# A hybrid decoder layer on one core: filler matmuls moved from the attention to the merge and the joint tiles behind it

## The chip, the cores and the metric

The kernel runs on one core of a Trainium2 chip. The metric is the device time of one execution in microseconds (us); the median of three runs is given. The core has a matmul engine (TensorE, here PE, with its weight loads shown as PEld), VectorE (DVE), ScalarE (ACT), GpSimd (POOL), SyncE (SP, which issues most transfers) and 16 DMA engines. PE accumulates into PSUM banks of 128 x 512 fp32; DVE and ACT read them from there. Each engine works through its own instructions in order and waits on semaphores for the others.

## The reference

The reference is one layer of a decoder for 1024 tokens and 1024 channels: an RWKV-7 path and a sparse attention path side by side, merged by sigmoid gates, then a SwiGLU FFN with 2816 hidden channels (22 tiles of 128) and a final RMSNorm. Cut to what matters here:

```
u    = rmsnorm(x, norm1_g);  proj = u @ w_in
y_a  = rwkv7_mix(...);       y_b  = dsa_attention(...)
merged = g_a * (y_a @ w_o_rwkv) + g_b * (y_b @ w_o_att)
h = x + merged @ w_out
z_gate, z_up = split(rmsnorm(h, norm2_g) @ w_ffn_in)
h = h + (silu(z_gate) * z_up) @ w_ffn_out
out = rmsnorm(h, normf_g)
```

## The kernel before

**Products.** Every fp32 operand is split into a rounded high part and a rest (`split`, L116: ACT makes the high part in L117, DVE subtracts it in L118). A product is the sum hi x hi + hi x lo + lo x hi, so an output tile of 128 channels x 512 tokens with eight blocks of 128 channels in is 24 matmuls. `mm3` (L138) issues them in the order of L143, L144, L148 and yields the number of matmuls after each few. `mm3_last` (L152) does several tiles at once and keeps the last input block for the end. Weights come by SP into the ring `wst` (three buffers), and their parts into `whi` and `wlo` (two each). The PSUM pool `acc` has three banks, the pool `mix` five. The ring `tmp` has four buffers of 128 x 512.

**Halves.** The tokens are worked on in two halves of 512. The second half is late: its attention has to end before its merge can start. The first half's FFN is therefore used as filler beside the second half's attention.

**The filler.** `fill` is a queue of generators. `pump(n)` adds n to a credit and takes steps from the queue until the credit is used up; each step takes off the number of matmuls it yielded. A generator that has just yielded stands still there, and what it would do next (to read its PSUM banks, for example) is issued only when it is pumped again. `run_over` runs a generator and pumps -n for each negative yield. PE's order is the order of the program, written out by hand in this way. The other engines are ordered by a planner, which works with estimated times, takes the earlier place in the program first, and puts rushed weights (`weights` with `rush`) ahead.

**The order around the change.** After the second RWKV half, 130 matmuls of filler are pumped. Then `attend(1)` runs over four pairs of heads with four blocks of 128 queries, 16 units. Per unit and head of the pair it makes the logits (L1082, reduced by DVE in L1084, exponential in L1087), transposes them (`turn`, L1096, copied by ACT in L1098) one unit later, and multiplies with the values (L1106) two units later. Each step yields a number that is pumped. At the end the sums go through DRAM (`close2` to `close4`: the transfer to d_s in L1131, back in L1137, the product L1142, the store to d_yb in L1143), with 6 pumped ahead of each step.

Then `merge(1)` loads both paths' results from DRAM (L1201), splits them, pumps 30, multiplies with w_o and the gates, pumps 10, multiplies with w_out into the residual h (L1236) and sums its squares (`Rms.add`, L250). It ends there for the second half.

The filler in this stretch is `ffn(0, ...)`: two groups of eight hidden tiles (`ffn_in`, 48 matmuls each, and then `ffn_out`, 192 matmuls, with the add of L1321 that reads each bank). While the second group's `ffn_out` runs, `scaled` multiplies the first half's z by its row of the norm, one block of 128 channels at a time (L1443, L1444, split, store to d_z in L1446).

**The joint tiles.** The last six hidden tiles are done by `joint` for both halves at once, with a scheme that needs seven block products where the plain way needs eight: sums and differences of weights (`s1` to `s4`, the ring `sw`) meet sums and differences of the two halves' activations. With h normed for the second half (L1540) and the first half's z read back from d_z (`old`, L1549), the mixed operands are T1 (L1556), T2 (L1571), T3 (L1570), B22 and T4 (L1580, L1581), each split into hi and lo. The first rows (`m1`, `m2`) need only the first half. Each tile j of six issues seven `product`s of 12 matmuls (L1505, L1506, L1508): Y with T1; m1 of tile j + 2; X with T2; Y with B22; X with T3; m2 of tile j + 2; X with T4. Copies by ACT (L1591 for m5, L1598 for u2) and adds by DVE (L1602, L1609) read the banks between products that go on in the same bank. What is left of the filler is issued in one go ahead of the first rows (`run(*fill)`).

**The output.** `reload` brings the joint tiles' results back for the first half. The second half's FFN becomes the filler (`ffn(1, ...)`), 48 are pumped, `ffn_out(0, ..., JOINT, sq0)` adds the last product of the first half, 60 more, `norm_out` writes the first half's output, and the rest of the filler and the second half's last product (`finish_out`) follow.

Of the kernel before, what the change touches and what calls it, by code (L numbers as in the profile page):

```python
# [27 lines left out]
JOINT = 2  # L28
# [22 lines left out]
def block_kernel(ctx: ExitStack, tc: tile.TileContext, ins: dict, outT: bass.AP, outR: bass.AP, stop=None, dbg=None):  # L51
# [126 lines left out]
    def pump(n):  # L178

        credit[0] += n  # L180
        while credit[0] > 0 and fill:
            try:
                credit[0] -= abs(next(fill[0]))
            except StopIteration:
                fill.popleft()
        if not fill:
            credit[0] = 0
# [857 lines left out]
    def attend(half, p, bias):  # L1045
# [112 lines left out]
        for i in range(len(units) + 2):  # L1158
            if i < len(units):
                hp, bi = units[i]  # L1160
                if i == 0:
                    kqv[hp] = load(hp)
                    load_q(hp, 0)
                    load_q(hp, 1)
                if bi == 2 and hp < 3:
                    kqv[hp + 1] = load(hp + 1, sms[hp][:, 0, :] if half else None)
                    load_q(hp + 1, 0)
                    load_q(hp + 1, 1)
                if bi == 0:
                    sms[hp] = smp.tile([128, 4, 2], F32, tag="sm", name="sm", bufs=3)  # L1170
                Ls[i] = []
            for e in range(2):
                if i < len(units):
                    Ls[i].append(logits(hp, bi, e, kqv[hp], sms[hp]))
                    yield 5 if half else (bi + 3) // 2
                if 0 <= i - 1 < len(units):
                    ptss.setdefault(i - 1, []).append(turn(units[i - 1][1], Ls[i - 1][e]))
                    yield 4 if half else (units[i - 1][1] + 3) // 2
            if i >= 2:
                hp2, bi2 = units[i - 2]  # L1180
                if bi2 == 0:
                    pys[hp2] = mix()
                values(bi2, ptss.pop(i - 2), kqv[hp2], pys[hp2])
                if bi2 == 3:
                    ri = close1(sms[hp2])
                yield 4 if half else bi2 + 1
                if bi2 == 3:
                    closing.append((2, hp2, ri))
                elif closing:
                    close(closing)  # L1190
# [5 lines left out]
    def merge(half, zp, zs, between=None):  # L1196
        yt = yhi, ylo = act_tiles(zp, "y", ("s0", "s1"))
        mt = act_tiles(zp, "m", ("s2", "s3"))
        for j in range(8):
            t = ylo[:, j, :].bitcast(F32)  # L1200
            SY.dma_start(t, (d_ya if j < 4 else d_yb)[half][j % 4])  # L1201
            split(yhi[:, j, :], ylo[:, j, :], t)
        yield -30
        for d in range(8):
            w = weights(ins["w_o"][d])
            ga, gb = tmp(), tmp()
# [218 lines left out]
    def ffn(half, zp, zs, tags, after=None):  # L1425

        for gi in range(JOINT):
            f = act_tiles(zp, "f", tags)
            yield from ffn_in(f, zs, gi)
            side = iter(after() if after and gi == JOINT - 1 else ())  # L1430
            for i, n in enumerate(ffn_out(half, zp, f, gi)):
                yield n
                if i % 2:
                    next(side, None)
            for _ in side:
                pass

# [20 lines left out]
    def parts(t):  # L1458
        return [t[:, k, :] for k in range(4)], [t[:, 4 + k, :] for k in range(4)]

    def joint(z0, zp0, zs1, zp1, md):


        g0, gn = GROUPS[JOINT]
# [65 lines left out]

        yield ahead
        h, sq = zs1
        sq.columns()
        pump(10)
        row = sq.row()
        pump(16)
        b11, b21 = ([[x[:, k, :] for k in ks] for x in z0] for ks in (range(4), range(4, 8)))

        def normed(k):
            V.scalar_tensor_tensor(h[:, k, :], h[:, k, :], par[:, P_N2 + k:P_N2 + k + 1], row,  # L1540
# [6 lines left out]
        def old(k):  # L1547
            t = tmp()
            SY.dma_start(t, d_z[k])  # L1549
            return t  # L1550

        t1, T1 = pair(zp1, "s2")
        for k in range(4):
            normed(k)
            x = old(k)
            V.tensor_tensor(x, h[:, k, :], x, op=ALU.subtract)  # L1556
            split(t1[:, k, :], t1[:, 4 + k, :], x)
        run(*fill)
        fill.clear()
        with tc.high_priority():  # L1560
            first_rows(0)
            first_rows(1)
        for j in range(2):
            m1(j)
            m2(j)
        (t2, T2), (t3, T3) = pair(zp1, "s3"), pair(zp0, "s2")
        for k in range(4):
            normed(4 + k)
            x, y = tmp(), old(k)
            V.tensor_tensor(x, h[:, 4 + k, :], h[:, k, :], op=ALU.subtract)  # L1570
            V.tensor_tensor(y, y, x, op=ALU.add)  # L1571
            split(t2[:, k, :], t2[:, 4 + k, :], y)
            split(t3[:, k, :], t3[:, 4 + k, :], x)
        b22, B22 = pair(zp1, "s1")
        for k in range(4):
            split(b22[:, k, :], b22[:, 4 + k, :], h[:, 4 + k, :])
        t4, T4 = pair(zp0, "s0")
        for k in range(4):
            x = old(4 + k)
            V.tensor_tensor(x, x, t2[:, k, :].bitcast(F32), op=ALU.subtract)  # L1580
            V.tensor_tensor(x, x, t2[:, 4 + k, :].bitcast(F32), op=ALU.subtract)  # L1581
            split(t4[:, k, :], t4[:, 4 + k, :], x)

        for j in range(gn):
            nxt, far = j + 1 < gn, j + 2 < gn
            if far:
                first_rows(j + 2)
            Y = acc()
            product(Y, w[j]["s1"], T1, True)
            m5 = tmp()  # L1590
            A.activation(m5, Y, AF.Copy)  # L1591
            if nxt:
                s1(j + 1)
            if far:
                m1(j + 2)
            product(X[j], w[j]["s2"], T2, False)
            u2 = md.tile([128, HT], F32, tag="u2", name="u2")
            A.activation(u2, X[j], AF.Copy)  # L1598
            if nxt:
                s2(j + 1)  # L1600
            product(Y, w[j]["s4"], B22, False)
            V.tensor_tensor(u2, u2, Y, op=ALU.add)  # L1602
            t = tmp()
            A.activation(t, u2, AF.Tanh, scale=0.5)
            if nxt:
                s4(j + 1)
            V.scalar_tensor_tensor(t, t, 1.0, u2, op0=ALU.add, op1=ALU.mult)
            product(X[j], w[j]["s3"], T3, False)
            V.tensor_tensor(m5, X[j], m5, op=ALU.add)  # L1609
            if nxt:  # L1610
                s3(j + 1)
            if far:
                m2(j + 2)
            V.scalar_tensor_tensor(t, m5, 0.5, t, op0=ALU.mult, op1=ALU.mult)
            SY.dma_start(d_f[1][j], t)
            product(X[j], w[j]["a22"], T4, False)
            V.scalar_tensor_tensor(f0[j], X[j], 0.5, f0[j], op0=ALU.mult, op1=ALU.mult)
            SY.dma_start(d_f[0][j], f0[j])
        t, B12 = pair(zp1, "s2")
        for k in range(4):  # L1620
            split(t[:, k, :], t[:, 4 + k, :], h[:, k, :])
        yield [Planes(*(a + b)) for a, b in zip(B12, B22)]

    def reload(half, f):
        for j in range(GROUPS[JOINT][1]):
# [85 lines left out]
    sb.close()  # L1711
    (sz1, zp1), zs1, sq0 = opened("right", "zp1"), [], []
    smd, md = opened("right", "md")
    stage_j = joint(z0[0], zp0, zs1, zp1, md)
    run_over(merge(1, zp1, zs1, next(stage_j)))
    z1 = next(stage_j)
    smd.close()
    fj = act_tiles(zp0, "f", ("s2", "s0"))
    reload(0, fj)
    fill.append(ffn(1, zp1, [z1, None], ("s3", "s0")))  # L1720
    pump(48)
    run_over(ffn_out(0, zp0, fj, JOINT, sq0))
    pump(60)
    run_over(norm_out(0, sq0[0]))
    pump(300)
    sz0.close()
# [88 lines left out]
```

## Time and profile before

| what | value |
|---|---|
| median of three runs | 1767.33 us (1766.26 to 1770.13) |
| the profiled execution | 1774.1 us, of which its span is 1772.2 us |
| mean granted PE clock | 0.984 |
| DMA | 253.45 MB in 148034 packets, 143 GB/s |
| second attention, first logits to last values | 980.65 to 1136.42 us |
| second merge, first to last dense matmul | 1153.67 to 1253.28 us |
| joint tiles, first row to the last product | 1278.67 to 1410.76 us |
| last product of the first half | 1421.64 to 1474.01 us |

Times within the profile are counted from the start of the span. In a timeline row the first number is the start, the second the length; a row may stand for several instructions (x4), and square brackets hold the idle time of the engine before it and what ended it. The length of a matmul is that of its way through the array, and the next one starts before it is over: the distance of the starts is what counts. In a row of the windows view stand the stretch, its length, the busy time and the number of instructions of each engine, the granted PE clock (1.00 is full), the DMA share and GB/s.

### The profile page before, as it was taken

The numbers are of one execution on the slowest core, as the hardware profiler recorded it, in microseconds if no ns is written. First come the engines' busy times: TensorE is split into PE (matmuls) and PEld (weight loads), VectorE is DVE, ScalarE is ACT, GpSimd is POOL, SyncE is SP. The second block draws the span as 40 slices with busy tenths as digits, with TensorE's granted clock in tenths as the row PEclk, the third lists the DMA queues.
The fourth block names the chain that finished last, engine by engine and source line by source line (L and its number), as shares of the span: only waits on it lengthen the run. The fifth ranks groups of instructions, "written<-read, shape, count | busy, mean of one in ns | idle before, by whom it ended". The sixth has DMA issues, their size and how long they took to land.

```text
span 1772.2 us, 26689 instructions
## 1 busy us (share of the span) xinstructions
PE 1708.6 (96%) x10000; PEld 1400.1 (79%) x10000; DVE 1147.6 (65%) x2238; ACT 871.4 (49%) x1685; POOL 104.5 (6%) x127
## 2 busy tenths in 40 slices
PE   8999999999999999999999999999989879999998
PEld 7888888888878777787878888767768757888887
DVE  6789899865577578678857555665686444433334
ACT  5365997543555888654243555433343332322322
POOL 0000000010022110001002110000000000000001
PEclk9999999999999999999999999999989999999999
DMA  5542344445376336632347553556522433353363
GB/s 212 184 133 78 108 110 144 146 129 155 111 220 183 114 122 200 202 108 93 115 127 214 147 155 102 177 186 203 171 77 86 162 111 122 126 170 112 112 192 104
DMA packets 148034, 253.45 MB, mean 143 GB/s; under 512 B 49681, under 2 KB 71889, under 8 KB 147777
## 3 DMA queue, kind: packets, MB, share of 16 engines
q1 hardware_dynamic: 123824, 176.53, 31.9%
q10 hardware_dynamic: 16128, 48.60, 8.5%
q0 software_dynamic: 7952, 26.61, 5.6%
q8 instruction: 79, 1.29, 0.3%
q14 instruction: 51, 0.41, 0.1%
HBM read 193.45 MB, written 58.25 MB: 142 GB/s over the span
## 4 chain that ended last, share of the span: by engine, by line
PE 54%; DVE 7%; DMA 6%; ACT 3%; issue 2%; POOL 1%; SPq 0%; ACTq 0%; DVEq 0%; POOLq 0%
PE acc L143 13%; PE acc L144 12%; PE acc L148 12%; PE acc L161 2%; DVE wlo L118 2%; PE mix L1082 2%; PE mix L1106 2%; PE mix L1096 2%; PE mix L1505 1%; PE mix L1508 1%; PE mix L1506 1%; DMA wst<-in_w_fo 1%; DMA wst<-in_w_ffn_in 1%; ACT whi L117 1%; DMA d_h<-tmp 1%
## 5 line engine op out<-in xcount | busy, mean ns | idle before, releaser
L118 DVE TENSOR_TENSOR wlo<-wst,whi 128x1024 fp32r<-128x1024 f32 (+1 forms) x203 | 247.5, 1220 | 252.7 <-ACT whi L117 131.4
L117 ACT ACTIVATE whi<-wst 128x1024 fp32r<-128x1024 f32 (+1 forms) x203 | 212.6, 1048 | 245.7 <-PE acc L144 196.3
L143 PE MATMUL acc<-u1hi,whi 128*128 128x512 f32 x320 | 127.9, 400 | 0.0
L144 PE MATMUL acc<-u1lo,whi 128*128 128x512 f32 x320 | 125.1, 391 | 0.0
L143 PE MATMUL acc<-u0hi,whi 128*128 128x512 f32 (+1 forms) x320 | 122.8, 386 | 0.0
L144 PE MATMUL acc<-u0lo,whi 128*128 128x512 f32 (+1 forms) x320 | 121.3, 382 | 0.0
L143 PE MATMUL acc<-fhi,whi 128*128 128x512 f32 x234 | 95.0, 406 | 12.6 <-DVE h L1321 12.5
L143 PE MATMUL acc<-s,whi 128*128 128x512 f32 x256 | 100.8, 394 | 2.1 <-DVE h L1321 2.1
L144 PE MATMUL acc<-s,whi 128*128 128x512 f32 x256 | 100.6, 393 | 0.0
L143 PE MATMUL acc<-zhi,whi 128*128 128x512 f32 x240 | 96.8, 403 | 0.0
L144 PE MATMUL acc<-zlo,whi 128*128 128x512 f32 x240 | 94.3, 393 | 0.0
L144 PE MATMUL acc<-flo,whi 128*128 128x512 f32 x234 | 93.7, 400 | 0.0
L148 PE MATMUL acc<-u1hi,wlo 128*128 128x512 f32 x320 | 81.8, 395 | 0.0
L148 PE MATMUL acc<-u0hi,wlo 128*128 128x512 f32 (+1 forms) x320 | 78.6, 384 | 0.0
L997 ACT ACTIVATE junkl<-kept,z 128x1024 int8<-128x1024 int16 (+1 forms) x64 | 69.4, 1084 | 4.7 <-DVE kept L966 4.4
L1087 ACT ACTIVATE L<-L,mx 128x128 f32<-128x128 f32 (+7 forms) x64 | 49.5, 774 | 43.8 <-DVE mx L1084 43.3
L143 PEld LDWEIGHTS acc<-u1hi,whi 128*128 128x128 f32 x320 | 60.1, 188 | 12.5 <-issue 0.9
L143 PEld LDWEIGHTS acc<-u0hi,whi 128*128 128x128 f32 x320 | 60.2, 188 | 11.9 <-issue 0.4
L144 PEld LDWEIGHTS acc<-u1lo,whi 128*128 128x128 f32 x320 | 60.2, 188 | 11.3
L144 PEld LDWEIGHTS acc<-u0lo,whi 128*128 128x128 f32 x320 | 60.2, 188 | 11.0
L148 PEld LDWEIGHTS acc<-u1hi,wlo 128*128 128x128 f32 x320 | 58.9, 188 | 12.5 <-issue 0.9
L148 PEld LDWEIGHTS acc<-u0hi,wlo 128*128 128x128 f32 x320 | 58.1, 188 | 11.9 <-issue 0.7
(429 smaller groups left out, 3975.7 us busy)
## 6 DMA issues: line engine op xcount, KB each, us to landing
wst<-in_w_ffn_in SPq DMA_DIRECT2D x61, 512.0 KB, 3.8
wst<-in_w_in ACTq DMA_DIRECT2D x36, 512.0 KB, 4.2
wst<-in_w_in SPq DMA_DIRECT2D x27, 512.0 KB, 3.9
wst<-in_w_fo SPq DMA_DIRECT2D x25, 512.0 KB, 4.0
k<-d_k POOLq DMA_DIRECT2D x24, 512.0 KB, 8.3
h<-in_xT SPq DMA_DIRECT2D x32, 256.0 KB, 5.2
d_g<-tmp ACTq DMA_DIRECT2D x32, 256.0 KB, 3.5
tmp<-d_g SPq DMA_DIRECT2D x32, 256.0 KB, 3.6
```

The lines of the kernel that those rows point to most:

```text
L117: A.activation(hi, x, AF.Copy)
L118: V.tensor_tensor(lo, x, hi.bitcast(F32), op=ALU.subtract)
L143: T.matmul(ps, whi[:, wk + k, :], ahi[:, ak + k, tok], start=k == 0, stop=False)
L144: T.matmul(ps, whi[:, wk + k, :], alo[:, ak + k, tok], start=False, stop=False)
L148: T.matmul(ps, wlo[:, wk + k, :], ahi[:, ak + k, tok], start=False, stop=k == nk - 1)
L161: T.matmul(ps, w[:, k, :], a[:, k, tok], start=k == 0 and j == 0, stop=k == nk - 1 and j == 2)
L997: A.activation(junka[:, :n], y, AF.Sign, bias=z[:, i:i + 1], accum_out=cnt[:, i:i + 1])
L1082: T.matmul(ps[:, :w], q[bi // 2][:, e, bi % 2 * 128:bi % 2 * 128 + 128], k[:, i, e, c:c + w], start=i == 0, stop=i == 1)
L1087: A.activation(L[:, :n], L[:, :n], AF.Exp, scale=-1.0, bias=last, accum_out=sm[:, bi, e:e + 1])
L1096: T.transpose(ps[:, j * 128:(j + 1) * 128], L[:, (c + j) * 128:(c + j + 1) * 128], ident)
L1106: T.matmul(py[64 * e:64 * e + 64, bi * 128:(bi + 1) * 128], v[:, j, 64 * e:64 * e + 64], pts[e][j // 4][:, j % 4, :], start=j == b, stop=j ...
L1505: T.matmul(ps, whi[:, k, :], hi[k], start=opens and k == 0, stop=False, skip_group_check=True)
```

## The change

The change moves filler matmuls and operand building; no arithmetic is changed, but that one subtraction per block (`less`) is done twice.

- In the second half's attention the yields fall from 5, 4 and 4 to 4, 3 and 3.
- The second merge pumps 56 instead of 30 while its operands are loaded.
- `scaled` takes a step at each yield of `ffn_out` instead of every second.
- In `joint`, 14 matmuls stand ahead of the column sums (none before), 14 instead of 10 between them and the row, 4 instead of 16 behind it. T2 and B22 are built right behind T1, ahead of the filler that is left; T3 and T4 are built in tile 0 behind its first product. The operand B12 is built in the last tile, which makes the second half's FFN the filler, and 8 of its matmuls go ahead of the last product.
- Behind `joint`, 136 matmuls are pumped instead of 48 ahead of the first half's last product, and 48 instead of 60 behind it. The credit is set to zero at two places.

```diff
-                    yield 5 if half else (bi + 3) // 2
+                    yield 4 if half else (bi + 3) // 2
...
-                    yield 4 if half else (units[i - 1][1] + 3) // 2
+                    yield 3 if half else (units[i - 1][1] + 3) // 2
...
-                yield 4 if half else bi2 + 1
+                yield 3 if half else bi2 + 1
...
-        yield -30
+        yield (-30, -56)[half]
...
-            for i, n in enumerate(ffn_out(half, zp, f, gi)):
+            for n in ffn_out(half, zp, f, gi):
                 yield n
-                if i % 2:
-                    next(side, None)
+                next(side, None)
...
-    def joint(z0, zp0, zs1, zp1, md):
+    def joint(z0, zp0, zs1, zp1, md, after):
...
-        sq.columns()
-        pump(10)
-        row = sq.row()
-        pump(16)
-        b11, b21 = ([[x[:, k, :] for k in ks] for x in z0] for ks in (range(4), range(4, 8)))
...
+        def less(k):
+            x = tmp()
+            V.tensor_tensor(x, h[:, 4 + k, :], h[:, k, :], op=ALU.subtract)
+            return x
+
+        pump(14)
+        sq.columns()
+        pump(14)
+        row = sq.row()
+        pump(4)
         t1, T1 = pair(zp1, "s2")
         for k in range(4):
             normed(k)
             x = old(k)
             V.tensor_tensor(x, h[:, k, :], x, op=ALU.subtract)
             split(t1[:, k, :], t1[:, 4 + k, :], x)
+        t2, T2 = pair(zp1, "s3")
+        for k in range(4):
+            normed(4 + k)
+            y, x = old(k), less(k)
+            V.tensor_tensor(y, y, x, op=ALU.add)
+            split(t2[:, k, :], t2[:, 4 + k, :], y)
+        b22, B22 = pair(zp1, "s1")
+        for k in range(4):
+            split(b22[:, k, :], b22[:, 4 + k, :], h[:, 4 + k, :])
         run(*fill)
         fill.clear()
+        credit[0] = 0
...
         for j in range(2):
             m1(j)
             m2(j)
-        (t2, T2), (t3, T3) = pair(zp1, "s3"), pair(zp0, "s2")
-        for k in range(4):
-            normed(4 + k)
-            x, y = tmp(), old(k)
-            V.tensor_tensor(x, h[:, 4 + k, :], h[:, k, :], op=ALU.subtract)
-            V.tensor_tensor(y, y, x, op=ALU.add)
-            split(t2[:, k, :], t2[:, 4 + k, :], y)
-            split(t3[:, k, :], t3[:, 4 + k, :], x)
...
+
+        def rest():
+            t3, T3 = pair(zp0, "s2")
+            for k in range(4):
+                split(t3[:, k, :], t3[:, 4 + k, :], less(k))
+            t4, T4 = pair(zp0, "s0")
+            for k in range(4):
+                x = old(4 + k)
+                V.tensor_tensor(x, x, t2[:, k, :].bitcast(F32), op=ALU.subtract)
+                V.tensor_tensor(x, x, t2[:, 4 + k, :].bitcast(F32), op=ALU.subtract)
+                split(t4[:, k, :], t4[:, 4 + k, :], x)
+            return T3, T4
...
             product(Y, w[j]["s1"], T1, True)
             m5 = tmp()
             A.activation(m5, Y, AF.Copy)
+            if j == 0:
+                T3, T4 = rest()
+            if not nxt:
+                t, B12 = pair(zp1, "s2")
+                for k in range(4):
+                    split(t[:, k, :], t[:, 4 + k, :], h[:, k, :])
+                after([Planes(*(a + b)) for a, b in zip(B12, B22)])
...
             product(X[j], w[j]["s3"], T3, False)
             V.tensor_tensor(m5, X[j], m5, op=ALU.add)
+            if not nxt:
+                pump(8)
...
-        t, B12 = pair(zp1, "s2")
-        for k in range(4):
-            split(t[:, k, :], t[:, 4 + k, :], h[:, k, :])
-        yield [Planes(*(a + b)) for a, b in zip(B12, B22)]
+        yield
...
-    z1 = next(stage_j)
+    next(stage_j)
     smd.close()
     fj = act_tiles(zp0, "f", ("s2", "s0"))
     reload(0, fj)
-    fill.append(ffn(1, zp1, [z1, None], ("s3", "s0")))
+    credit[0] = 0
+    pump(144 - 8)
+    run_over(ffn_out(0, zp0, fj, JOINT, sq0))
     pump(48)
-    run_over(ffn_out(0, zp0, fj, JOINT, sq0))
-    pump(60)
     run_over(norm_out(0, sq0[0]))
```

More of the change, by code (lines that the diff above doesn't have):

```diff
@@ L1557, in joint @@
             split(t1[:, k, :], t1[:, 4 + k, :], x)
+        t2, T2 = pair(zp1, "s3")
[7 more added lines that the diff above has]
+            split(b22[:, k, :], b22[:, 4 + k, :], h[:, 4 + k, :])
         run(*fill)
         fill.clear()
+        credit[0] = 0
+        b11, b21 = ([[x[:, k, :] for k in ks] for x in z0] for ks in (range(4), range(4, 8)))
         with tc.high_priority():
@@ L1565, in joint @@
             m2(j)
-        (t2, T2), (t3, T3) = pair(zp1, "s3"), pair(zp0, "s2")
-        for k in range(4):
-            normed(4 + k)
-            x, y = tmp(), old(k)
-            V.tensor_tensor(x, h[:, 4 + k, :], h[:, k, :], op=ALU.subtract)
-            V.tensor_tensor(y, y, x, op=ALU.add)
-            split(t2[:, k, :], t2[:, 4 + k, :], y)
-            split(t3[:, k, :], t3[:, 4 + k, :], x)
-        b22, B22 = pair(zp1, "s1")
-        for k in range(4):
[L1576 to L1582, printed above, removed]
+        def rest():
[9 more added lines that the diff above has]
+            return T3, T4
         for j in range(gn):
@@ L1618, in joint @@
             SY.dma_start(d_f[0][j], f0[j])
-        t, B12 = pair(zp1, "s2")
-        for k in range(4):
-            split(t[:, k, :], t[:, 4 + k, :], h[:, k, :])
-        yield [Planes(*(a + b)) for a, b in zip(B12, B22)]
+        yield
     def reload(half, f):
@@ L1713, in block_kernel @@
     smd, md = opened("right", "md")
-    stage_j = joint(z0[0], zp0, zs1, zp1, md)
+    stage_j = joint(z0[0], zp0, zs1, zp1, md,
+                    lambda z1: fill.append(ffn(1, zp1, [z1, None], ("s3", "s0"))))
     run_over(merge(1, zp1, zs1, next(stage_j)))
-    z1 = next(stage_j)
+    next(stage_j)
     smd.close()
```

## Prediction

> **What bounds the kernel now.** I read the page's busy shares first, then the waits of the matmul engine (engine and line, what it waited for: us in total, times, longest), then its timeline around the longest of these waits.
>
> ```profile
> span 1772.2 us, 26689 instructions
> PE 1708.6 (96%) x10000; PEld 1400.1 (79%) x10000; DVE 1147.6 (65%) x2238; ACT 871.4 (49%) x1685; POOL 104.5 (6%) x127
> ```
> ```profile
> PE acc L143 <- DVE h L1321: 14.6, 8, 2.1
> PE acc L143 <- ACT yhi L117: 5.0, 1, 5.0
> PE mix L256 <- DVE sacc L250: 3.4, 1, 3.4
> PE mix L1505 <- ACT u L1598: 3.3, 1, 3.3
> PE acc L1505 <- ACT tmp L1591: 2.6, 1, 2.6
> PE mix L1505 <- DVE tmp L1609: 1.6, 2, 0.8
> ```
>
> PE is busy 96% of the span, so a matmul that only changes place costs nothing. What can be won is PE's idle time, and the slow matmuls behind it. Five of these six rows (not the u one) lie where the change moves something. The windows view (stretch; length and busy us of PE, PEld, DVE, ACT, POOL; granted clock) shows the slow part, and first a stretch without any idle time:
>
> ```profile
> 980.65:1136.42 155.77, 155.77 (x1104) 129.92 (x1102) 93.20 (x205) 88.29 (x169) 16.27 (x30) 1.00 0.48 131
> 1154.00:1161.00 7.00, 7.00 (x17) 4.78 (x17) 5.69 (x9) 3.97 (x7) 0.00 (x0) 0.55 0.94 302
> 1257.00:1263.00 6.00, 6.00 (x20) 5.02 (x20) 1.99 (x3) 0.00 (x0) 1.02 (x1) 0.52 0.77 246
> 1264.04:1315.46 51.42, 46.75 (x188) 36.84 (x186) 46.56 (x72) 24.27 (x38) 0.00 (x0) 0.90 0.36 117
> 1305.00:1312.00 7.00, 7.00 (x21) 5.50 (x20) 4.40 (x8) 2.35 (x4) 0.00 (x0) 0.61 0.00 0
> 1387.00:1393.00 6.00, 5.40 (x12) 3.70 (x12) 4.38 (x7) 2.11 (x4) 0.00 (x0) 0.55 0.44 131
> 1421.64:1474.01 52.37, 37.80 (x145) 28.64 (x144) 21.30 (x29) 14.28 (x21) 0.00 (x0) 0.93 0.29 88
> ```
>
> After the idle times of 5.0, 3.4, 2.6 and 3.3 us the granted clock stands near 0.55 for some 6 us. PE's timeline (start, length, what, idle time before) gives the unit and the places:
>
> ```profile
> 1136.42 0.50 PE L143 MATMUL acc<-fhi,whi 128*128 128x512 f32 x1
> 1148.29 0.39 PE L144 MATMUL acc<-flo,whi 128*128 128x512 f32 x1
> 1153.67 0.79 PE L143 MATMUL acc<-yhi,whi 128*128 128x512 f32 x1 [4.99 <-ACT yhi L117]
> 1160.32 0.40 PE L143 MATMUL acc<-yhi,whi 128*128 128x512 f32 x1
> 1242.24 0.39 PE L143 MATMUL acc<-mhi,whi 128*128 128x512 f32 x1
> 1247.68 0.39 PE L143 MATMUL acc<-mhi,whi 128*128 128x512 f32 x1
> 1256.68 1.84 PE L256 MATMUL mix<-kc,sacc 128*128 128x2 f32 x8 [3.39 <-DVE sacc L250]
> 1262.76 0.40 PE L143 MATMUL acc<-fhi,whi 128*128 128x512 f32 x1
> 1304.27 0.80 PE L1505 MATMUL acc<-s,sw 128*128 128x512 f32 x1 [2.56 <-ACT tmp L1591]
> 1407.86 0.50 PE L1505 MATMUL mix<-s,sw 128*128 128x512 f32 x1 [0.79 <-DVE tmp L1609]
> ```
>
> **The unit.** From 1242.24 to 1247.68 PE runs one output tile of 24 dense matmuls: 5.44/24 = 0.227 us each. One credit of the filler is one such matmul.
>
> **The change part by part.**
>
> *1. Attention, 80 matmuls fewer beside it.* Each of the 16 units gives two logits, two turn and one values yield, each one lower: 5 x 16 = 80 matmuls, 18.1 us of PE, come later. Until 1136.42 PE has no idle time in 155.77 us, with DVE busy 93.20 (60%) and ACT 88.29 (57%). Over 155.77 - 18.1 = 137.7 us that would be at most 68% and 64%, less what the 80 matmuls bring of their own splits. So the cost is between 0 and the whole 18.1 us with its cold clock (rival C). I take 2 us, near the row without idle time, for a few waits on a PSUM bank of the transposes.
>
> *2. The second merge's first wait.* Idle 4.99; then 14 matmuls take 1160.32 - 1153.67 = 6.65 us instead of 3.17, so 3.5 more: 8.5 us. What PE waits for is a chain of transfers that starts when the last values end:
>
> ```profile
> 1139.89 0.29 SPq L1131 DMA_DIRECT2D d_s<-tmp  x1
> 1149.37 0.32 SPq L1143 DMA_DIRECT2D d_yb<-tmp  x1
> 1149.75 1.85 SPq L1201 DMA_DIRECT2D ylo<-d_ya  x4
> ```
>
> From 1136.42 to 1153.67 this is 17.25 us. Its cover was 18 credits of the closing steps and 30 of the merge (with overshoot 52 matmuls). It becomes 18 + 56 = 74 credits, 16.8 us: 0.5 us stay uncovered, too short for the clock as far as these rows show. Gain 8.0, bounds -2 (rival B) to 8.5. Behind the lengthened yield on SP's queue lie only the later stores and weight loads, whose landing no wait above names.
>
> *3. The norm of the second half.* Idle 3.39, then 6.08 us at clock 0.52, of which some 2.9 are slowness: 6.3. Now 14 matmuls (3.17 us) stand ahead of L256 and leave 0.2. Gain 6.1, bounds 3 to 6.3. The 14 between the column sums and the spread are 3.2 us at full clock; before, 12 cold ones covered that step, without a wait.
>
> *4. Mixed operands.* 184 dense matmuls stand from 1264.04 to 1315.46 (64 filler, 48 first rows, 72 of j=0 ahead of its last product): 41.7 us of 51.42, so 9.7 lost. In that stretch DVE is busy 46.56: it is the bound. Its steps follow each other at 0.60 us, and a weight tile's costs 1.2:
>
> ```profile
> 1295.32 0.68 DVE L118 TENSOR_TENSOR s<-tmp,s 128x512 fp32r<-128x512 f32 x1
> 1295.92 0.68 DVE L1570 TENSOR_TENSOR tmp<-h 128x512 f32<-128x512 f32 x1
> L118 DVE TENSOR_TENSOR wlo<-wst,whi 128x1024 fp32r<-128x1024 f32 (+1 forms) x203 | 247.5, 1220 | 252.7 <-ACT whi L117 131.4
> ```
>
> The filler has some 80 - 26 - 14 = 40 matmuls more here (26 went to the merge, 14 ahead of L256), 224 in all, 50.8 us. They bring 40/24 of an add and a weight split, 40/24 x (0.6 + 1.2) = 3.0 us of DVE; the subtraction of less() is now done twice, 4 x 0.60 = 2.4. DVE needs 46.56 + 5.4 = 52.0 us against 50.8: 1.2 short without a gap, 6.1 short with the 4.9 us of gaps of before. What improves is the order: T2 and B22 stand ahead of the drained filler, and m5 takes its tmp buffer ahead of T3 and T4, so the copy of L1591 need not wait behind them. The d_z loads of T2 go ahead of the filler's d_h loads on SP and in the four tmp buffers. I take 3.0 us idle and the cold stretch of the 2.56 us row, 7.00 x 0.39 = 2.7: 5.7 left of 9.7, gain 4.0, bounds -2 (6.1 idle, two cold stretches) to 9.7.
>
> The Trainium skill (TensorE: Matmul & The Clock Gate, section Part 1: The HAM clock gate) says that the clock falls after an idle window of about 3.4 us. By that rule the 3.0 us left here would cost no clock, and the sum below would be 19.6 instead of 16.9; the trace disagrees, since 2.56 us were enough for 0.61.
>
> *5. The last joint tile.* Eight matmuls of the second FFN cover the 0.79 us ahead of the last product: 0.8, bounds 0 to 0.8. The four splits of B12 were already done at this place by ACT. The 3.3 us wait on u stays: ACT stood in front of a weight whose load shares the DMA with eight h loads.
>
> ```profile
> 1373.28 4.39 POOL L1303 DMA_DIRECT2D h<-d_h  x8 [113.45 <-PE mix L1508]
> 1385.32 1.06 ACT L117 ACTIVATE whi<-wst 128x1024 fp32r<-128x1024 f32 x1 [5.38 <-DMA wst<-in_w_ffn_in]
> ```
>
> *6. 144 filler matmuls instead of 48 ahead of the first half's last product, 48 instead of 60 behind it.* In the last stretch of the windows, 144 matmuls (32.6 us) take 52.37: 19.7 lost, 14.6 of it the waits on L1321. The cause is that the suspended filler keeps two of three acc banks:
>
> ```profile
> 1475.17 0.68 DVE L1285 SCALAR_TENSOR_TENSOR tmp<-tmp,acc 128x512 f32<-128x512 f32 x1
> ```
>
> L1285 reads the bank of the filler's first tile only after the whole product. 8 + 136 = 144 = 3 x 48 stops it again between the last matmul and these reads, now of the third tile: the same two banks are held, the same eight waits come. Gain 0. The reload's cover grows from 11 to 31 us, but no wait on it was in the list. The scaled steps (rescaling z) at each yield instead of every second have no price by themselves; they now lie in the merge's 56 (rival B).
>
> **The sum.** 8.0 + 6.1 + 4.0 + 0.8 - 2.0 = 16.9 us. Against the profiled execution, 1774.1 us with 1772.2 of span, this gives 1757.2. That execution lies 6.8 above the median of 1767.33, by which I forecast 1767.3 - 16.9 = **1750.4 us**.
>
> **The rivals.**
>
> *A. DVE overload in part 4.* The operands take DVE and the tmp buffers from the filler's adds (L1321), and PE waits for acc as well. For it: 52.0 us of work against 50.8. Against it: in the old trace the adds found their places between the T1 steps (L1556).
>
> ```profile
> 1270.49 0.68 DVE L1556 TENSOR_TENSOR tmp<-h,tmp 128x512 f32<-128x512 f32 x1
> ...
> 1271.75 0.68 DVE L1321 TENSOR_TENSOR tmp<-tmp,acc 128x512 f32<-128x512 f32 x1
> ```
>
> With it part 4 gives -2: 1756.4.
>
> *B. The scaled steps delay y.* They now come only when the last FFN tile is done, about 6 us after attention: 8 x 3 x 0.60 = 14.4 us of DVE in the time in which y arrives. If DVE's order has them all ahead of y's splits, y is there some 7 us after the cover ends, with 3.5 of cold clock: part 2 gives -2, 1760.4. Against it: y's splits stand ahead of them in the program.
>
> *C. Attention needed the cover (the slower one).* If a unit can't run faster than its old 155.77/16 = 9.7 us, PE idles the 18.1 us there in short pieces, and these cool the clock as in the stretch of part 6, where 14.6 us idle cost 19.7: 18.1 x 1.35 = 24.5. It decides from 77% of that, where the 18.9 us of parts 2 to 5 are used up. 1767.3 - 18.9 + 24.5 = 1772.9. Against it: no idle time at all before, DVE and ACT at 60%. The Trainium skill (the same page, section A second HAM failure mode: psum-queue depth-cycling) has this as a rule: PE that idles shortly between groups while it cycles through banks falls back in clock. The old attention shows none of it at 1.00; the stretch of part 6 does.
>
> *D. Held banks come free in part 6:* 19.7 more, 1730.7.
>
> *E. The wait on u goes too,* 3.3 and 6.00 x 0.45 = 2.7: 1744.4.
>
> *F. The change does not do what it says:* the waits come again at other places, within 0.2% of before.
>
> **How the numbers follow.** Chances: forecast 0.40, A 0.17, B 0.15, C 0.08, D 0.04, E 0.10, F 0.06. The range takes in forecast, A, B, E with their bounds: 1742 to 1765, 0.82. Faster by over 0.2% (about 3.5 us, what a measurement here can tell from no change): forecast, A, B, D, E, 0.85 after 0.01 off for mixtures; within 0.2%: F and that, 0.07; slower: C, 0.08.
>
> **What would show it.** Right: no 5 us wait on yhi and no 3.4 us wait on sacc, clock 1.00 behind both, units of attention about 8.6 us apart, eight waits on L1321 still there. Wrong: waits of PE on mx, L or pt in attention (C); y's splits behind scaled steps on DVE (B); waits on L1321 ahead of the first rows, or on s or sw in j=0 beyond 3 us (A).

## The result, and the profile after

The changed kernel takes 1781.26 us (median of 7 runs, 1777.74 to 1794.05), the kernel before 1769.74 us beside it (median of 7 runs, 1764.21 to 1770.23). The ratio is 1.0082, with a 95% interval of 1.0054 to 1.0109: it is **slower** by 0.8%, clear of the noise, where faster by 17 us was forecast. The profiled execution of the changed kernel has a span of 1779.4 us, 7.2 more than the one before. That one took 1774.1 us, 4.4 above its median, so the two traces show 7.2 us of a loss of 11.5 us by the medians and 14.5 us by the ratio; the rest is not located.

The page of the changed kernel begins almost as before. PE has less busy time (1699.8 us, 1708.6 before), and still the span is longer: PE's idle time rose from 63.6 to 79.6 us.

```profile
span 1779.4 us, 26713 instructions
PE 1699.8 (96%) x10000; PEld 1395.9 (78%) x10000; DVE 1149.3 (65%) x2242; ACT 869.2 (49%) x1685; POOL 104.3 (6%) x127
```

The waits of PE in the changed kernel (engine and line, what it waited for: us in total, times, longest) name it. L1504 is here the matmul of `product`:

```profile
PE acc L143 <- DVE tmp L1321: 25.7, 2, 12.9
PE acc L143 <- DVE h L1321: 13.1, 7, 2.1
PE acc L143 <- ACT whi L117: 7.3, 11, 1.9
PE mix L1504 <- ACT u L1615: 2.5, 1, 2.5
PE mix L1504 <- DVE tmp L1626: 1.7, 1, 1.7
PE mix L1504 <- ACT s L117: 1.2, 1, 1.2
PE mix L256 <- DVE sacc L250: 1.2, 1, 1.2
```

The wait on yhi has gone, that on sacc has shrunk from 3.4 to 1.2, and the one on m5's copy has gone. New is the first row: two waits, of 12.86 and 12.83 us, for a PSUM bank that an add of L1321 has yet to read. The waits for weights (`whi`) were 4.0 us in ten waits before; the longest of the eleven here, 1.92 us, stands at 1138.12, right ahead of the first of the two. The windows view of both kernels (before, then after) cuts the time from the first logits to the end at the same five events: the first dense matmul with y, the column sums (L256), the first rows, the end of the joint tiles, the end. The second column is the length, and the number in the first round brackets is that of PE's instructions:

```profile
980.65:1153.60 172.95, 168.03 (x1157) 139.62 (x1155) 100.22 (x214) 92.69 (x176) 16.27 (x30) 1.00 0.51 144
1153.60:1256.60 103.00, 95.77 (x392) 74.34 (x392) 60.65 (x80) 35.33 (x46) 0.00 (x0) 0.96 0.58 182
1256.60:1278.60 22.00, 21.92 (x92) 18.43 (x93) 15.64 (x24) 7.43 (x11) 1.02 (x1) 0.86 0.67 221
1278.60:1410.70 132.10, 122.56 (x506) 98.23 (x505) 87.61 (x131) 49.23 (x79) 4.38 (x8) 0.94 0.31 101
1410.70:1772.20 361.50, 338.90 (x1533) 282.88 (x1532) 149.75 (x193) 104.26 (x135) 10.32 (x15) 0.98 0.42 133
```
```profile
980.75:1152.40 171.65, 156.43 (x1102) 129.43 (x1100) 101.09 (x219) 95.44 (x181) 16.07 (x30) 0.96 0.48 137
1152.40:1254.95 102.55, 97.20 (x408) 76.86 (x408) 57.65 (x76) 30.74 (x38) 0.00 (x0) 0.98 0.58 179
1254.95:1298.00 43.05, 30.15 (x132) 24.79 (x133) 27.53 (x42) 13.11 (x18) 1.02 (x1) 0.84 0.59 183
1298.00:1422.75 124.75, 119.05 (x514) 97.02 (x513) 80.25 (x118) 45.29 (x73) 4.37 (x8) 0.99 0.31 102
1422.75:1779.40 356.65, 335.56 (x1526) 280.14 (x1524) 149.48 (x193) 103.31 (x135) 10.30 (x15) 0.99 0.42 134
```

A raw difference of two lengths misleads, because matmuls moved from one stretch to another. So each difference is corrected by 0.227 us for each matmul more or fewer:

| stretch | length, difference | matmuls | corrected |
|---|---|---|---|
| first logits to the product with y | -1.30 | -55 | +11.2 |
| to the column sums | -0.45 | +16 | -4.1 |
| to the first rows | +21.05 | +40 | +12.0 |
| joint tiles | -7.35 | +8 | -9.2 |
| to the end | -4.85 | -7 | -3.3 |

Three stretches gained 16.6 us. Two lost 23.2, and each holds one of the new waits. PE's timeline shows them:

```profile
1152.48 0.77 PE L143 MATMUL acc<-yhi,whi 128*128 128x512 f32 x1 [12.86 <-DVE tmp L1321]
1255.01 1.02 PE L256 MATMUL mix<-kc,sacc 128*128 128x2 f32 x8 [1.16 <-DVE sacc L250]
1285.38 0.76 PE L143 MATMUL acc<-fhi,whi 128*128 128x512 f32 x1 [12.83 <-DVE tmp L1321]
```

**The first wait.** What did DVE do meanwhile? Its timeline (L1442 and L1443 are here `scaled`'s two steps):

```profile
1136.53 1.32 DVE L118 TENSOR_TENSOR ylo<-ylo,yhi 128x512 fp32r<-128x512 f32 x2 [0.80 <-ACT yhi L117]
...
1140.63 2.49 DVE L118 TENSOR_TENSOR ylo<-ylo,yhi 128x512 fp32r<-128x512 f32 x4
1143.04 1.28 DVE L1442 TENSOR_TENSOR tmp<-zhi,zlo 128x512 f32<-128x512 f32 x2
...
1149.67 1.28 DVE L1443 TENSOR_TENSOR tmp<-tmp,row 128x512 f32<-128x512 f32 x2
...
1151.65 0.68 DVE L1321 TENSOR_TENSOR tmp<-tmp,acc 128x512 f32<-128x512 f32 x1
```

The first four blocks of y, all that the first product with y needs, were split by 1137.85, the other four by 1143.12. PE could not multiply them, for its next bank still held a finished filler tile whose add came at 1151.65, behind the scaled steps. The load of that add's other operand stood behind them as well, on SP's queue and in the four tmp buffers:

```profile
1148.39 0.37 SPq L1315 DMA_DIRECT2D tmp<-d_h  x1
```

So both DVE's order and a late operand could be the cause; e1 and e5 test them. DVE was not overloaded in general (65% of the span). From 1143 to 1151 it worked on scaled steps, for which nobody waited yet.

**The second wait.** SP's queue and DVE ahead of the first rows:

```profile
1255.86 0.43 SPq L1315 DMA_DIRECT2D tmp<-d_h  x1
1282.25 2.73 SPq L1315 DMA_DIRECT2D tmp<-d_h  x3
```
```profile
1272.46 0.68 DVE L1548 TENSOR_TENSOR tmp<-h 128x512 f32<-128x512 f32 x1
...
1283.95 0.68 DVE L118 TENSOR_TENSOR s<-tmp,s 128x512 fp32r<-128x512 f32 x1
1284.56 1.87 DVE L1321 TENSOR_TENSOR tmp<-tmp,acc 128x512 f32<-128x512 f32 x3
```

From 1272 to 1284.6 DVE built T2 and B22 (L1548 is `less`) with one weight split between, and only then did it make the adds of the last filler tiles. PE stood from 1272.5 on. By the order of the loads and the adds, the operand of the first of these adds, the one that frees PE's next bank, had been issued at 1255.86, 28.7 us ahead of it: here the order on DVE held the bank, not the operand. The operands of the later adds were issued only from 1282.25 on.

### The profile page after: what moved, and what is told of

Its sections match the earlier page's. It is cut to its first block, busy times and chain, and to the rows that moved or that the text cites. A ratio compares the mean times of both kernels' runs of the same rounds, so it can differ in the third digit from the quotient of the medians.

```text
span 1779.4 us, 26713 instructions
## 1 busy us (share of the span) xinstructions
PE 1699.8 (96%) x10000; PEld 1395.9 (78%) x10000; DVE 1149.3 (65%) x2242; ACT 869.2 (49%) x1685; POOL 104.3 (6%) x127
## 4 chain that ended last, share of the span: by engine, by line
PE 78%; DVE 9%; DMA 6%; ACT 3%; issue 2%; POOL 1%; SPq 0%; ACTq 0%; DVEq 0%; POOLq 0%
PE acc L143 18%; PE acc L144 18%; PE acc L148 17%; PE acc L161 3%; DVE wlo L118 2%; PE mix L1106 2%; PE mix L947 2%; PE mix L1082 2%; PE mix L1096 2%; DMA d_h<-tmp 1%; ACT whi L117 1%; PE mix L1507 1%; PE mix L1505 1%; PE mix L1504 1%; PE mix L143 1%
## 5 line engine op out<-in xcount | busy, mean ns | idle before, releaser
L118 DVE TENSOR_TENSOR wlo<-wst,whi 128x1024 fp32r<-128x1024 f32 (+1 forms) x203 | 247.9, 1222 | 245.1 <-ACT whi L117 116.2
L117 ACT ACTIVATE whi<-wst 128x1024 fp32r<-128x1024 f32 (+1 forms) x203 | 212.4, 1048 | 288.6 <-PE acc L144 229.7
L143 PE MATMUL acc<-fhi,whi 128*128 128x512 f32 x234 | 94.4, 404 | 26.8 <-DVE tmp L1321 12.8
L143 PEld LDWEIGHTS acc<-fhi,whi 128*128 128x128 f32 x234 | 44.9, 192 | 39.8 <-issue 27.9
L143 PEld LDWEIGHTS acc<-u1hi,whi 128*128 128x128 f32 x320 | 60.3, 189 | 12.7 <-issue 0.9
L143 PEld LDWEIGHTS acc<-u0hi,whi 128*128 128x128 f32 x320 | 60.2, 188 | 11.9 <-issue 0.4
```

Of the source, the lines that this page charges most:

```text
L117: A.activation(hi, x, AF.Copy)
L118: V.tensor_tensor(lo, x, hi.bitcast(F32), op=ALU.subtract)
L143: T.matmul(ps, whi[:, wk + k, :], ahi[:, ak + k, tok], start=k == 0, stop=False)
```

## The experiments

Lines move with the edits: the add L1321 is L1328, and `product` lies between L1504 and L1513. All edits are to the changed kernel, except that of e10. Each ratio is to runs of the kernel before beside it. By the intervals of the table, a difference of two ratios is uncertain by some 0.0025 to 0.004, 4 to 7 us.

| run | median us | ratio to before, 95% interval |
|---|---|---|
| changed kernel | 1781.26 | 1.0082 (1.0054 to 1.0109) |
| e1 | 1780.51 | 1.0065 (1.0047 to 1.0083) |
| e2 | 1782.82 | 1.0079 (1.0052 to 1.0107) |
| e3 | 1777.24 | 1.0056 (1.0035 to 1.0077) |
| e4 | 1764.51 | 0.9972 (0.9951 to 0.9992) |
| e5 | 1770.84 | 1.0010 (0.9997 to 1.0023) |
| e6 | 1758.58 | 0.9930 (0.9909 to 0.9951) |
| e7 | 1764.66 | 0.9979 (0.9960 to 0.9997) |
| e8 | 1744.68 | 0.9843 (0.9811 to 0.9874) |
| e9 | 1755.04 | 0.9903 (0.9888 to 0.9918) |
| e10 | 1749.86 | 0.9874 (0.9855 to 0.9892) |
| e11 | 1745.87 | 0.9841 (0.9813 to 0.9869) |
| e12 | 1743.74 | 0.9830 (0.9802 to 0.9858) |

### e1: the d_h loads of the first two adds ahead of their product

```diff
+        early = []
+        if half == 0 and gi == JOINT - 1:
+            for d in range(2):
+                early.append(tmp())
+                SY.dma_start(early[d], d_h[half][d])
...
+            elif d < len(early):
+                t = early[d]
```

> The changed kernel, but the second group's output product takes its two residual tiles (the loads from d_h for the adds of L1321) ahead of its first matmuls, so ahead of the eight scaled steps in the tmp ring. Theory tmp: the first wait on L1321 (12.9 us) is there because these loads stand behind the eight scaled steps in the four tmp buffers. Then it falls below 3 us with no cold clock behind it, the second one (12.8 us) stays, and the time falls from 1781 to between 1766 and 1772. Rival DVE: the add itself stands behind the scaled steps in DVE's order whatever the load does. Then the load lands early, the wait stays above 8 us, and the time stays between 1776 and 1783.

The first add, with its operand early, came at 1138.60, ahead of the scaled steps, and PE ran the first product with y on the bank that it freed. The wait only moved to the next bank. The second add's operand was issued at 1135.72, and this add still came behind the scaled steps (L1450 here), as SP's and DVE's timelines of e1 show:

```profile
1135.72 0.38 SPq L1313 DMA_DIRECT2D tmp<-d_h  x1
```
```profile
1138.60 0.68 DVE L1328 TENSOR_TENSOR tmp<-tmp,acc 128x512 f32<-128x512 f32 x1
...
1155.91 1.29 DVE L1450 TENSOR_TENSOR tmp<-tmp,row 128x512 f32<-128x512 f32 x2
1157.12 0.68 DVE L1328 TENSOR_TENSOR tmp<-tmp,acc 128x512 f32<-128x512 f32 x1
```

PE's wait was 14.24 us, and the time can't be told from that of the changed kernel. So a late operand has a part in the first add, but to bring it early does not help: for the second bank it is DVE's order.

### e2: scaled steps at every second yield again

```diff
-            for n in ffn_out(half, zp, f, gi):
+            for i, n in enumerate(ffn_out(half, zp, f, gi)):
                 yield n
-                next(side, None)
+                if i % 2:
+                    next(side, None)
```

> The changed kernel, but scaled takes a step at every second yield as before, so six steps instead of eight stand ahead of the first two adds. Theory tmp: a step holds up the loads by about 2.3 us, so the first wait falls from 12.9 to about 8 us and the time to between 1774 and 1778. Rival: the pace of the steps has no part in it, the wait stays at 12 to 13 us and the time at 1779 to 1783.

```profile
1153.52 0.76 PE L143 MATMUL acc<-yhi,whi 128*128 128x512 f32 x1 [10.84 <-DVE tmp L1321]
```

The wait fell by 2 us, between the 8 us of the theory and the 12 of the rival, and the time can't be told from that of the changed kernel. At half the pace some of the scaled steps still stand between the splits and the first add in DVE's timeline (1146.50 to 1152.70). The pace alone does not decide; what stands ahead of the adds does.

### e3: T2 and B22 behind the first rows again

The block that builds T2 and B22 is moved, unaltered, behind the loop of `m1` and `m2`, where the kernel before had it.

> The changed kernel, but T2 and B22 are built behind the first rows, as before the change. Theory tmp: the second wait on L1321 (12.8 us) comes from T2's eight tmp buffers ahead of the filler's loads; it falls below 3 us, the first one stays, and a wait on T2 in tile 0 of 4 to 9 us comes back with its cold clock: 1769 to 1776. Rival: the filler's adds are late because there are 40 more filler matmuls behind the row, whatever is built there; a wait of more than 8 us on L1321 stays, and the time lies above 1778.

```profile
PE acc L143 <- DVE tmp L1321: 13.2, 1, 13.2
```

One of the two long waits is left, the first. The second was made by T2 and B22 standing ahead of the drained filler's adds. The gain by the ratios, 0.0026 or 4.6 us, is less than the 12.83 removed, and the noise does not separate it from none; the time, 1777.24, lies above the range of the theory. Some of it was lost again in the first joint tile: between 1303 and 1325 e3 has 6.0 us of waits on s and on the add of L1626, where the changed kernel has 1.5 in its first tile (on s); the rest was not located.

### e4: the attention's cover back

```diff
-                    yield 4 if half else (bi + 3) // 2
+                    yield 5 if half else (bi + 3) // 2
...
-                    yield 3 if half else (units[i - 1][1] + 3) // 2
+                    yield 4 if half else (units[i - 1][1] + 3) // 2
...
-                yield 3 if half else bi2 + 1
+                yield 4 if half else bi2 + 1
...
-        yield (-30, -56)[half]
+        yield -30
```

> The changed kernel with the old yields in attention and the old 30 in the merge, so the 80 matmuls are back beside attention; all of the joint part and the output part is kept. Theory tmp: the filler is far enough along that both waits on L1321 fall below 3 us each; the old wait on yhi of 5 us is back with its cold clock; T2 and the rest are late by 3 to 8 us because DVE loses 9 us of cover: 1762 to 1769. Rival: T2 and B22 ahead of the filler delay the adds here too, a wait on L1321 of more than 5 us stays between the row and the first rows: above 1771.

```profile
1158.53 0.80 PE L143 MATMUL acc<-yhi,whi 128*128 128x512 f32 x1 [5.15 <-ACT yhi L117]
```

Both long waits are gone, and the wait on yhi is back. In this version what is left of the change is faster than before (interval below 1). So the hold-back, in the order that the change gives it, costs 1.0082 - 0.9972 = 0.0110, 19.5 us: it is what puts the adds behind the other work.

### e5: the adds first, with the hold-back kept

```diff
-            for n in ffn_out(half, zp, f, gi):
+            for i, n in enumerate(ffn_out(half, zp, f, gi)):
                 yield n
-                next(side, None)
+                if i >= 12:
+                    next(side, None)
+                    next(side, None)
```

> The changed kernel, but scaled starts behind the first two adds of the second group's output product (from the thirteenth yield on, two steps per yield). Theory order: DVE works in the order of the program, and the eight scaled steps stood ahead of the add that frees the bank. Then the first wait on L1321 falls from 12.9 us to below 3, the second one of 12.8 stays, and the time falls from 1781 to between 1764 and 1769. Rival supply: DVE or the banks are simply overloaded at that place, so the wait moves to another add or to y: a wait above 6 us stays within 20 us of there, and the time is above 1774.

```profile
1142.65 0.50 PE L143 MATMUL acc<-yhi,whi 128*128 128x512 f32 x1 [1.05 <-DVE tmp L1321]
1273.26 0.76 PE L143 MATMUL acc<-fhi,whi 128*128 128x512 f32 x1 [12.83 <-DVE tmp L1321]
```

The scaled steps begin only with the thirteenth yield, behind the first two adds in the program, so neither these adds nor the loads of their operands stand behind them. The first wait falls from 12.86 to 1.05 us, the second stays to the hundredth, and the time falls by 0.0072, 12.7 us, a little less than expected. This settles the first wait: the scaled steps ahead of the adds made it.

### e6: e5, and T2 and B22 behind the drained filler

To e5's edit one is added: the block of T2 and B22 is moved to behind `run(*fill)`, still ahead of the first rows.

> The same with T2 and B22 built behind the filler's rest, ahead of the first rows. Theory order: the second wait on L1321 goes as well (below 2 us), since the filler's adds now stand ahead of T2 in the program; T2 is late in tile 0 by less than 4 us: 1750 to 1758. Rival: DVE has too little time between the row and tile 0 (52.0 us of work for 50.8 us), and what is won at the filler is lost on T2, T3 and T4 with more than 8 us: above 1762.

Both long waits are gone; the second was worth 0.0080 against e5, 14 us. The waits for the mixed operands (s, of L117 and L118) rise from 1.5 us in the changed kernel to 2.7, the longest of them

```profile
1308.33 0.53 PE L1506 MATMUL mix<-s,sw 128*128 128x512 f32 x1 [1.18 <-ACT s L117]
```

The longest is as long as that of the changed kernel. So with the adds ahead, the operands are still nearly in time. What step 4 wanted (T2 ahead of the first rows) was right, and its place one block too early.

### e7: held banks set free

A suspended generator of `ffn_in` has issued all matmuls of its tile but not the reads of the two banks. This edit issues those reads ahead of the tile's last yield; the yields of the second product each come one step later by it, and the matmuls keep their order:

```diff
-            pg, pu = acc(), acc()
+            pg, pu, last = acc(), acc(), 0
...
-                yield from mm3(pu, weights(src[1]), z)
+                n = 0
+                for m in mm3(pu, weights(src[1]), z):
+                    if n:
+                        yield n
+                    n = m
+                last = n
...
+            if last:
+                yield last
```

> The changed kernel, but the filler's FFN tile does its reads of the two banks ahead of its last yield instead of behind it, with the matmuls in the same order, so that a filler that stands still holds no bank. Theory banks: the seven waits of 1.8 to 2.1 us on h L1321 in the first half's last product (13.1 us) vanish, with them the stretch of low clock there: 1762 to 1768; both long waits stay. Rival: that product is bound by its weight splits or by the adds themselves, waits of more than 1 us stay at each tile, and the time stays above 1775.

```profile
PE acc L143 <- DVE tmp L1328: 26.6, 2, 13.8
```

The row of seven waits on h is gone from the list, the two long waits are untouched, and the time falls by 0.0103, 18 us, for 13.1 us of waits.

### e8: e6 and e7 together

> All three edits together: scaled behind the adds, T2 and B22 behind the filler's rest, banks read ahead of the last yield. If the three causes are independent, the gains add up: 1781 less 14, 13 and 16 gives 1734 to 1744, faster than both kernels. If one only moves the wait of another, above 1750.

The three repairs add up: 0.0152 (e6) and 0.0103 (e7) are 0.0255, and 0.0239 was measured, 0.0252 in the repetition e12. The time, 1744.68, lies just above the expected range. The version is faster than both kernels.

### e9: e8 with the attention's cover back

The four yields of e4's diff are set back in e8.

> The version with all three edits of order and banks, but with the attention's yields 5, 4, 4 and the merge's 30 of the kernel before. Theory (once nothing stands in front of the adds, the 80 matmuls held back are worth the wait on yhi that they cover): that wait of some 5 us and its cold clock of 3.5 come back, so 8 us above the version with all three edits, near 1753. Rival (the hold-back brings nothing, since the short waits in the attention and a second gap take as much): within 3 us of that version, 1742 to 1748.

It is 0.0060 above e8, 10.6 us, near the theory's size, but not by the theory's wait. PE's and SP's timelines of e9:

```profile
1164.76 0.80 PE L143 MATMUL acc<-yhi,whi 128*128 128x512 f32 x1 [12.76 <-ACT yhi L117]
```
```profile
1148.09 0.28 SPq L1131 DMA_DIRECT2D d_s<-tmp  x1
```

With more filler beside the attention, the paired scaled steps fall into the closing steps of the attention. In the kernel before, the store of the sums was issued at 1139.89, 3.5 us after the last values (1136.42); here it is at 1148.09, 8.3 us after them (1139.79) and between two stores of d_z, and y is late by the difference. At 1322.59, in the joint tiles, PE waits 6.87 us for the add of L1635 (L1626 in the changed kernel), which e8 does not. So e9 does not measure the hold-back alone, and its agreement in size is no proof. It asked for a version with the attention's cover and the change's own pace of scaled steps: e11.

### e10: the kernel before, with held banks set free

The edit of e7, in the kernel before.

> The kernel before with one edit: the reads of an FFN tile's two banks are issued ahead of the tile's last yield, so that a suspended filler holds no bank. Theory (the held banks were a cost of the kernel before too): the eight waits on h of L1321, 14.6 us, go, and with their colder clock 16 to 17 us, as in the changed kernel: 1752 to 1753. Rival (in the kernel before something else then stands at this place, such as the reload of f): under 8 us, 1761 or more.

It gained 0.0126, 22.3 us, more than the 16 to 17 of the theory and far more than the rival's 8. The last row of the first half's last product stands at 1470.43 in the timeline of before (it began at 1421.64); in e10 it began at 1420.26:

```profile
1420.26 1.30 PE L161 MATMUL acc<-fhi,whi 128*128 128x512 f32 x5
...
1451.54 1.52 PE L148 MATMUL acc<-fhi,wlo 128*128 128x512 f32 x6
```
```profile
1420.26:1455.00 34.74, 34.74 (x155) 28.80 (x154) 22.50 (x31) 14.48 (x21) 0.00 (x0) 1.00 0.41 132
```

48.8 us became 31.3, without any idle time and at clock 1.00, where the stretch had 0.93 before. These are 17.5 us of the 22.3; the rest is not located. This one edit of the kernel before, with nothing of the change, is worth more than the change was forecast to bring.

### e11 and e12: is the hold-back worth anything?

e11 is the changed kernel with e4's diff and e7's diff, so the attention's cover and the pump of 30 are those of before. It needs neither e5's nor e6's edit, for e4 has no long wait on a bank. e12 is e8 once more, on the same chip. So the best version without the hold-back stands beside the best one with it.

> The changed kernel with the attention's yields and the merge's 30 of the kernel before, and with the bank reads ahead of the last yield; the rest of the change as it is. Theory (the parts for the norm, the mixed operands and the output are a gain, and the held banks another): ratio 0.997 - 0.010 to 0.997 - 0.013, so 0.984 to 0.987; no long wait on L1321, one wait of some 5 us on yhi, one of 1 to 3 us in tile 0. Rival (the gains lie in the same time, or the changed pace of the filler meets the closing steps of the attention, as in the version with two scaled steps per yield): 0.990 or more, with a wait on yhi above 8 us.

> The version with all three edits once more, beside the version before it in the list and the same runs of the kernel before. Theory (holding 80 matmuls back is worth some 8 us when nothing stands in front of the adds): 8 us below the version with the attention's yields of before. Rival (the other parts are what gains): within 3 us of it. A ratio of 0.981 to 0.988 is expected either way.

```profile
PE acc L143 <- ACT yhi L117: 5.9, 1, 5.9
```

The ratios are 0.9841 and 0.9830, the medians 2.1 us apart. By the six runs of each, the means differ by 2.0 us, with a 95% interval of -1.9 to 5.9: no difference is shown, and the theory's 8 us lies outside. So the rival holds: e11 keeps the wait on yhi, e12 has none, and still they take nearly the same time. Where e12 gives part of the 5.9 us back is seen in its timeline: around the arrival of y, PE waits in four pieces, 1.41 for weights (ACT), 0.43 for ylo, 1.67 for a bank (DVE) and 0.24 for weights again, 3.75 us in all. The remaining few us are spread over waits below 2 us and were not traced one by one.

## Why the prediction was wrong

**The failed steps are 2 and 4, both by the same assumption:** that PE, given enough filler, has a bank to go on in.

*Step 1 (attention, cost 2.0).* Right. First logits to the end of the last values took 138.7 us (980.82 to 1119.48) instead of 155.8: 17.1 of the 18.1 us came out, a cost of 1.0. Rival C, the only slower case that was given a chance, is false.

*Step 2 (first wait of the merge, gain 8.0, bounds -2 to 8.5).* Wrong: with the attention's 1.0 taken out, the stretch up to the product with y lost some 10 us (12.86 and 1.92 of new waits, less the 4.99 on yhi, and some short ones). "Its cover was 18 credits ... It becomes 18 + 56 = 74 credits, 16.8 us: 0.5 us stay uncovered" counted matmuls against the transfers of y. The transfers were covered (no wait on yhi is left). What the step did not ask is which DVE work frees the banks of those matmuls. With the group held back, its adds and the scaled steps came due in the same time, and the scaled steps went first, on DVE and, for the first add, in the tmp buffers too (e1). Rival B had the scaled steps as the culprit, but with y's splits as the victim, at -2. The splits were in fact not behind all of them; the banks were. e5 moves only these steps and takes 11.8 of the 12.86 us away.

*Step 3 (norm, gain 6.1, bounds 3 to 6.3).* The mechanism is right. The wait on sacc is 1.16 instead of 3.39, and the stretch behind it has clock 1.00 where 0.52 stood before:

```profile
1256.00:1263.00 7.00, 7.00 (x36) 5.89 (x36) 1.77 (x3) 1.66 (x2) 1.02 (x1) 1.00 0.88 290
```

The shorter wait is 2.2 us of the 4.1 that the second stretch of the table gained; most of the rest is the cold stretch at its start, 5 us at 0.61 where before had 7 at 0.55. The 2.9 us of the cold clock behind sacc were won in the third stretch, and are drowned there: the second wait, 12.83, and its own cold clock, 7.00 x 0.29 = 2.0, less 2.9 make 11.9 of the 12.0 lost. Gain 2.2 + 2.9 = 5.1, inside the bounds.

*Step 4 (mixed operands, gain 4.0, bounds -2 to 9.7).* Wrong in the sum, right for the tiles. In the joint tiles 9.2 us were won. Some 5.3 of them are this step's: the wait on m5's copy, 2.56, and its cold stretch, 2.7, are gone. Some 3.5 belong to the wait on u, 0.84 shorter and without its cold stretch of 2.7, which the sum did not have. But ahead of the first rows 12.0 were lost. "What improves is the order: T2 and B22 stand ahead of the drained filler" was itself the fault: the drained filler's adds stood behind them. Rival A named this victim (the adds of L1321), at 6 us, and held it unlikely by an old row in which an add found its place between the steps of T1. That row showed an add between two steps of T1; in the rows above no add stands between 1272.46 and 1284.56, 12.1 us. e3 moves only this block against the changed kernel, e6 only this block against e5, and both remove the wait.

*Step 5 (last joint tile, 0.8).* Right: in PE's timeline the last product follows the eight filler matmuls without idle time (1418.28 to 1420.10), where 0.79 stood before. The wait on u was said to stay; it did, at 2.46 instead of 3.30 us, and without the cold clock.

*Step 6 (output, gain 0).* Right in kind: seven waits instead of eight, 13.1 us instead of 14.6, and 3.3 us won. That held banks are their cause was argued then; e7 and e10 show it. Rival D's price for them, 19.7, stands beside 18 and 22.3 measured.

In short, steps 3 to 6 had 10.9 us of gain, and the three stretches that hold most of it gained 16.6; step 2's 8.0 became a loss, and step 4 brought a second one. Both waits were near to rivals, which alone would have cost 6 us (A) and 10 us (B) against the forecast, both still faster than before. The sign that was named for A, waits on L1321 ahead of the first rows, did come. A was sized by how much work DVE has (52.0 us against 50.8) and not by how long one uninterrupted run of work can keep a bank. B did count such a run, but against y's splits. Rival F had the waits come again at other places, as they did, but no longer than those that went. No rival had two waits of 12.8 us.

## What to carry to other kernels

When filler matmuls are moved, follow their banks too: for each one, find the read that frees its bank, and list what stands ahead of that read on its engine, and ahead of the load of its operand. A cover counted in matmuls lasts only as long as there are free banks: with three banks in `acc`, PE stood still at both long waits with the banks of three tiles not yet read. Reads that free a bank belong ahead of work that nobody waits for, and a generator must not be suspended between its last matmul and these reads: the latter alone was worth 1.3% in the kernel before.

## What the runs showed of the hardware

The granted clock was less regular than the idle times. In the windows of the changed kernel, behind the waits of 12.86, 12.83 and 2.46 us:

```profile
1152.00:1157.00 5.00, 4.52 (x13) 3.65 (x14) 1.62 (x3) 0.00 (x0) 0.00 (x0) 0.61 0.89 268
1285.00:1292.00 7.00, 6.62 (x22) 5.33 (x23) 1.43 (x3) 0.94 (x1) 0.00 (x0) 0.71 0.55 194
1400.00:1425.00 25.00, 23.26 (x102) 18.91 (x102) 12.13 (x19) 5.99 (x12) 0.00 (x0) 1.00 0.34 106
```

The waits of 12.8 us cost no more clock afterwards than the one of 2.56 did in the kernel before (0.61), and 2.46 us cost nothing here. The length of the idle time does not settle it: in e11 the same wait on u, 2.45 us at 1385.55, was followed by 0.72 over 6 us, and in e3 two successive waits of 2.06 us on h, at 1491.66 and 1499.68, by 0.72 and by 1.00. The Trainium skill (TensorE: Matmul & The Clock Gate, section Part 1: The HAM clock gate) describes a free-running window of some 3.4 us, in which such a difference could be a matter of phase; that 2.56 and 2.06 us were enough is below its figure, and no run here shows the phase itself. Its section A second HAM failure mode: psum-queue depth-cycling agrees with e10: with the short waits for banks gone, the same stretch rose from clock 0.93 to 1.00.
